# Latent attention: from a planned order to a fixed one

## The chip, the cores and the metric

The kernel runs on one core of a Trainium2 chip. The metric is the device time of one execution in microseconds (us).

## The reference, cut to what matters

The model is two blocks: an attention and recurrence block with its feed-forward part, and a second block of two layers (neighbourhood attention with a feed-forward part, then latent attention with a mixture of eight experts). The change lies in the latent attention, here for 256 tokens, 16 heads, 64 unrotated and 32 rotated dimensions of each query and key, 64 of each value:

```python
def _apply_rope(x, cos, sin):
    x1 = x[..., 0::2].astype(jnp.float32)
    x2 = x[..., 1::2].astype(jnp.float32)
    out = jnp.stack([x1 * cos - x2 * sin, x1 * sin + x2 * cos], axis=-1)
...
def _mla(h, w_down, q_norm, w_uq, kv_norm, w_ukv, w_o):
    down = h @ w_down
    c_q = _rmsnorm(down[..., :MLA_Q_LORA]) * q_norm
    c_kv = _rmsnorm(down[..., MLA_Q_LORA:MLA_Q_LORA + MLA_KV_LORA]) * kv_norm
    k_rope = down[..., MLA_Q_LORA + MLA_KV_LORA:]
    q = (c_q @ w_uq).reshape(B, S, MLA_HEADS, MLA_NOPE + MLA_ROPE)
    kv = (c_kv @ w_ukv).reshape(B, S, MLA_HEADS, MLA_NOPE + MLA_V)
    k_nope, v = kv[..., :MLA_NOPE], kv[..., MLA_NOPE:]
...
        s = (jnp.einsum('bqhd,bkhd->bhqk', qn, k_nope)
             + jnp.einsum('bqhr,bkr->bhqk', qr, k_rope)).astype(jnp.float32) * scale
        p = jax.nn.softmax(s, axis=-1).astype(v.dtype)
        return jnp.einsum('bhqk,bkhd->bqhd', p, v)
...
    return o @ w_o
```

## The kernel before

Matrices are multiplied as sums of three products: each float32 operand is split into a rounded high part (a copy on ScalarE) and the rest (a subtraction on VectorE). `split_to` does this for activations (L524), and `Stream.split` for weights (L98, L99): every weight slab of up to 128 x 1024 costs one ScalarE copy and one VectorE subtraction. `W.next()` hands out the next split slab and splits further ones ahead, into six buffers.

The 16 heads are treated in eight pairs, the 256 query rows in two tiles of 128 rows (`t`). For each pair the work is:

- `prepare`: for every second pair a projection of the queries of four heads (twelve matmuls of 384 columns into two `pb` banks, L486 to L489; copies to `qt` on ScalarE, L1149) and the rotation of their last 32 dimensions on VectorE (`turn`, L1068 to L1073, six instructions for each row tile). Then the keys of the pair (three matmuls, L1153 to L1155) and the transposes of the queries (four, L1162), both split with `split_to`.
- `scores`: six matmuls for each row tile into a `pa` bank (L699 to L701).
- `softmax_rows`, for each row tile: a row maximum for each head on VectorE (L643), the scaling of both (L644), the exponentials with their sums on ScalarE (L646), a reciprocal (L648) and a multiply for each head (L650) on VectorE.
- `turn_P`: eight transposes (L663) into `pb` and `pc` banks and two copies on ScalarE (L669).
- `pv`: eight matmuls (L676), split into `oT`.

`attention` writes these steps down in the order scores i, softmax i, prepare i + 2, turn i - 1, product with the values i - 1. Nothing holds the engines to that order: a planner orders the instructions of each engine by priority and by its own idea of when each can run, so that work of later steps and of other stages may be put between. In the stage of the experts the helper `in_order` ties the instructions of an engine to the order in which they are written; instructions written elsewhere may still be put between them. Behind the stage `out_proj` multiplies `oT` with the output weights: 96 matmuls of 512 columns that accumulate in all four `pa` banks. PSUM has four `pa` banks, two `pb` and two `pc`; `pbc` takes `pb` and `pc` in turn.

Of the kernel before, what the change touches and what calls it, by code (L numbers as in the profile page):

```python
# [19 lines left out]
S, D = 256, 1024  # L20
# [154 lines left out]
def consts():  # L175
# [8 lines left out]
    rope = np.stack([np.cos(ang), np.sin(ang)], 1).astype(np.float32)  # L184
# [4 lines left out]
def model(ctx: ExitStack, tc: tile.TileContext, A, out, cap=128):  # L189
# [443 lines left out]
    def softmax_rows(Ps, srcs, biases, scale):  # L633
# [4 lines left out]
        for i in range(n):  # L638
            if biases is not None:
                V.tensor_tensor_reduce(Ps[i], srcs[i], biases[i], scale=1.0, scalar=-3.0e38, op0=OP.add, op1=OP.max,  # L640
                                       accum_out=mx[:, i:i + 1])
            else:
                V.tensor_reduce(mx[:, i:i + 1], srcs[i], axis=AX.X, op=OP.max)  # L643
        V.tensor_scalar(mx, mx, -scale, None, OP.mult)  # L644
        for i in range(n):
            SC.activation(Ps[i], srcs[i] if biases is None else Ps[i], AF.Exp, bias=mx[:, i:i + 1], scale=scale,  # L646
                          accum_out=sums[:, i:i + 1])
# [8 lines left out]
    def turn_P(P, pt, causal, rev):  # L656
        for h in range(2):
            ps = pbc()
# [6 lines left out]
            if causal:  # L665
                V.tensor_copy(*run(pt[:, h, 0], ps[:, 0:256]))
                V.tensor_copy(*run(pt[:, h, 1, 128:256], p3[:, 1, 1]))
            else:
                SC.copy(*run(pt[:, h].rearrange("p k n -> p (k n)"), ps))  # L669
# [382 lines left out]
    with ExitStack() as ph:  # L1052
# [8 lines left out]
        SC.dma_start(rope, A["c_rope"].rearrange("(t p) u f -> p t u f", p=128))  # L1061
# [12 lines left out]

        with ExitStack() as ph2:
# [9 lines left out]
            for c0, c1, n in ((256, 384, 160), (0, 256, 256)):  # L1085
# [8 lines left out]
                for t in range(2):  # L1094
# [13 lines left out]
                    tmp = sm.tile([128, 4, 1, 16], F32, name="rt1")  # L1108
                    turn(dn[t][:, 384:416].rearrange("p (o n) -> p o n", o=1), 1, t, tmp)
# [27 lines left out]
        q = ph.enter_context(tc.tile_pool(name="mla2", bufs=2))  # L1137
        qTs = [pair(q, [128, 2, S], "qT") for _ in range(2)] + [(q3[:, 0], q3[:, 1])]
        qt = {}

        def prepare(i):
            if i % 2 == 0:
                w = W.next()
                acc = [[pb()], [pb()]]
                for kk in range(2):
                    tokmm(acc, cT, kk, w, kk == 0, kk == 1, halves=1, n=384, o=kk * 384)
                qt[0] = q.tile([128, 2, 4, 96], F32, name="qt")
                for t in range(2):
                    SC.copy(qt[0][:, t].rearrange("p h n -> p (h n)"), acc[t][0][:, :384])  # L1149
                    tmp = q.tile([128, 4, 4, 16], F32, name="rt4")  # L1150
                    turn(qt[0][:, t, :, 64:96], 4, t, tmp)
# [4 lines left out]
            k = kT[i % 3]  # L1156
            for h in range(2):
                split_to(k[0][0:64, h], k[1][0:64, h], ps[h * 64:h * 64 + 64, :256])
            pq = pbc()
            for h in range(2):  # L1160
                for t in range(2):
                    PE.transpose(pq[0:96, (h * 2 + t) * 128:(h * 2 + t + 1) * 128], qt[0][:, t, 2 * (i % 2) + h], ident)  # L1162
            qT = qTs[i % 3]
            split_to(qT[0][0:96], qT[1][0:96], pq[0:96].rearrange("p (h n) -> p h n", h=2))
            return qT, k
# [366 lines left out]
```

## Time and profile before

| | us |
|---|---|
| median of 3 runs | 1331.69 |
| lowest and highest of them | 1330.03 and 1334.1 |
| profiled execution, its own time | 1335.88 |
| span of the profiled execution | 1333.9 |
| TensorE busy in it | 1259.1 |
| VectorE busy in it | 1077.9 |
| ScalarE busy in it | 847.9 |

The profile is of one execution; its span is the time between its first and its last instruction. Times in it are us from the start of the span, and durations of single instructions are ns where a view says so. In the profile PE is TensorE's matmul, PEld its weight load, DVE VectorE, ACT ScalarE, POOL GpSimd, SP the engine that issues most loads. The latent attention lies between about 675 and 788 us of the span.

### The profile page before, as it was taken

How to read it: one execution, taken by the hardware profiler on the slowest of the kernel's cores; microseconds unless marked ns; L12 is line 12 of the kernel's file. 1: busy time of each engine (PE TensorE's matmuls, PEld its weight loads, DVE VectorE, ACT ScalarE, POOL GpSimd, SP SyncE). 2: the span in 40 equal slices, each digit the busy share in tenths (PEclk: the TensorE clock that was granted, in tenths of full speed). 3: DMA queues.
4: the chain of work that ended last, by engine and by line, in shares of the span. 5: the costliest groups of instructions: out<-in, count | busy, mean ns of one | idle time of the engine just before them, and what ended most of it. 6: DMA issues, size and time to landing. Idle time of an engine off the chain costs nothing. (4 is left out here: it accounts for less than half of the span.)

```text
span 1333.9 us, 20102 instructions
## 1 busy us (share of the span) xinstructions
PE 1259.1 (94%) x7459; PEld 1121.3 (84%) x7459; DVE 1077.9 (81%) x1761; ACT 847.9 (64%) x1354; POOL 36.2 (3%) x68
## 2 busy tenths in 40 slices
PE   7988999999999989999998988999999999999985
PEld 6966989999798779999987667889998988999873
DVE  6796699997787496878768867988888898888995
ACT  7874555555566554434447747777777787878872
POOL 4000000000100000000000020000000000000000
PEclk9999999999899989999979998999999999999997
DMA  9843599893685277899642145999999999999990
GB/s 329 301 142 125 150 386 338 294 323 111 203 271 174 80 284 260 315 382 346 226 140 91 30 141 190 390 362 353 369 380 348 354 378 377 336 355 390 376 347 34
DMA packets 190171, 359.56 MB, mean 270 GB/s; under 512 B 15460, under 2 KB 147970, under 8 KB 189937
## 3 DMA queue, kind: packets, MB, share of 16 engines
q1 hardware_dynamic: 187361, 351.70, 74.9%
q10 hardware_dynamic: 1584, 3.91, 0.7%
q0 software_dynamic: 1120, 2.58, 0.5%
q8 instruction: 61, 1.00, 0.3%
q14 instruction: 45, 0.37, 0.1%
HBM read 351.56 MB, written 7.06 MB: 269 GB/s over the span
## 5 line engine op out<-in xcount | busy, mean ns | idle before, releaser
L99 DVE TENSOR_TENSOR wlo<-raw,whi 128x1024 fp32r<-128x1024 f32 (+2 forms) x577 | 644.9, 1158 | 125.4 <-ACT whi L98 118.9
L98 ACT CAST whi<-raw 128x1024 fp32r<-128x1024 f32 (+2 forms) x577 | 557.5, 1003 | 115.8 <-PE pa L489 35.5
L1453 PE MATMUL pa<-wlo,xT 128*128 128x448 f32 x512 | 186.3, 364 | 3.3 <-DVE wlo L99 3.3
L1452 PE MATMUL pa<-whi,xT 128*128 128x448 f32 x512 | 188.4, 368 | 0.4 <-ACT whi L98 0.4
L1454 PE MATMUL pa<-whi,xT 128*128 128x448 f32 x512 | 185.5, 362 | 0.0
L289 DVE SCALAR_TENSOR_TENSOR acc<-raw,cact,acc 128x1024 f32<-128x1024 f32 x84 | 107.3, 1277 | 3.1 <-DMA raw<-in_w_ada_dram 2.9
L1453 PEld LDWEIGHTS pa<-wlo,xT 128*128 128x128 f32 x512 | 96.3, 188 | 10.9 <-DVE wlo L99 4.8
L1452 PEld LDWEIGHTS pa<-whi,xT 128*128 128x128 f32 x512 | 96.3, 188 | 7.4 <-ACT whi L98 0.7
L1454 PEld LDWEIGHTS pa<-whi,xT 128*128 128x128 f32 x512 | 96.1, 188 | 6.3
L486 PE MATMUL pb<-whi,hTh 128*128 128x512 f32 x224 | 88.6, 396 | 0.7 <-ACT hTh L524 0.7
L487 PE MATMUL pb<-wlo,hTh 128*128 128x512 f32 x224 | 88.8, 396 | 0.2 <-DVE wlo L99 0.2
L478 PE MATMUL pb<-hTh,whi 128*128 128x256 f32 x512 | 75.3, 291 | 0.3 <-ACT hTh L575 0.2
L478 PEld LDWEIGHTS pb<-hTh,whi 128*128 128x128 f32 x512 | 71.0, 197 | 5.1 <-ACT hTh L575 1.3
L478 PE MATMUL pb<-hTl,whi 128*128 128x256 f32 x512 | 72.9, 285 | 0.0
L478 PE MATMUL pb<-hTh,wlo 128*128 128x256 f32 x512 | 72.8, 286 | 0.0
L489 PE MATMUL pb<-whi,hTl 128*128 128x512 f32 x224 | 70.1, 395 | 1.6 <-DVE hTl L524 1.6
L486 PE MATMUL pa<-whi,fh 128*128 128x512 f32 x176 | 69.6, 395 | 0.0
L487 PE MATMUL pa<-wlo,fh 128*128 128x512 f32 x176 | 69.2, 393 | 0.0
L478 PEld LDWEIGHTS pb<-hTl,whi 128*128 128x128 f32 x512 | 66.9, 194 | 0.0
L478 PEld LDWEIGHTS pb<-hTh,wlo 128*128 128x128 f32 x512 | 66.8, 194 | 0.1
L478 PE MATMUL pc<-hTh,whi 128*128 128x256 f32 x448 | 63.8, 285 | 2.4 <-ACT whi L98 2.4
L478 PE MATMUL pc<-hTl,whi 128*128 128x256 f32 x448 | 63.7, 286 | 0.0
(433 smaller groups left out, 2081.4 us busy)
## 6 DMA issues: line engine op xcount, KB each, us to landing
raw<-in_moe_w_gu_dram SPq DMA_DIRECT2D x128, 896.0 KB, 7.6
raw<-in_moe_w_down_dram SPq DMA_DIRECT2D x56, 1024.0 KB, 6.7
raw<-in_w_ada_dram SPq DMA_DIRECT2D x48, 1024.0 KB, 7.5
raw<-in_w_up_dram SPq DMA_DIRECT2D x22, 1024.0 KB, 9.9
raw<-in_ffn_w_gu_dram SPq DMA_DIRECT2D x22, 1024.0 KB, 6.2
raw<-in_na_w_qkv_dram SPq DMA_DIRECT2D x12, 1024.0 KB, 5.0
raw<-in_w_down_dram SPq DMA_DIRECT2D x11, 1024.0 KB, 4.8
raw<-in_ffn_w_down_dram SPq DMA_DIRECT2D x11, 1024.0 KB
```

The costliest lines, as they stand in the source:

```text
L98: self.last = self.nc.scalar.copy(h, src)
L99: self.nc.vector.tensor_sub(l, src, h.bitcast(F32))
L289: V.scalar_tensor_tensor(ada_acc[0], raw, cact[:, k:k + 1], ada_acc[0], op0=OP.mult, op1=OP.add)
L478: PE.matmul(ps, lhsT=w[:, k], rhs=x[:, k], start=n + k == 0, stop=n == 2 and k == KD - 1)
L486: PE.matmul(acc[t][j][:, :n], lhsT=xh, rhs=ws[j][0], start=first, stop=False)
L487: PE.matmul(acc[t][j][:, :n], lhsT=xh, rhs=ws[j][1], start=False, stop=False)
L489: PE.matmul(acc[t][j][:, :n], lhsT=xl, rhs=ws[j][0], start=False, stop=last)
L1452: PE.matmul(ps, lhsT=xh, rhs=wh, start=k == 0, stop=False)
L1453: PE.matmul(ps, lhsT=xh, rhs=wl, start=False, stop=False)
L1454: PE.matmul(ps, lhsT=xl, rhs=wh, start=False, stop=k == KD - 1)
```

## The change

The stage gets a function of its own, `pairs`, whose instructions on TensorE, ScalarE and VectorE are tied to the order in which they are written (`in_order`). That order differs from before: the P of the pair before is turned ahead of the scores of the next, in two `pa` banks; the product with the values stands last. The queries of four heads are projected and rotated four pairs ahead of their scores, that is two pairs ahead of their own transposes (the first two projections before the loop). The maxima of both row tiles stand ahead of the normalising, one instruction for two heads, already negated; the scale is multiplied into the queries when they are split. The reciprocals and multiplies of tile 0 stand before the preparation of pair i + 2, those of tile 1 behind it, and then the rotation and the rests of the splits. A rotation is three instructions for both row tiles, with tables that hold each cosine twice and each sine with both signs; GpSimd writes the sines out for four heads. P has three buffers in a pool of its own, and the turned P is written into P's own tile.

```diff
-    rope = np.stack([np.cos(ang), np.sin(ang)], 1).astype(np.float32)
+    rope = np.stack([np.repeat(np.cos(ang), 2, -1), np.stack([-np.sin(ang), np.sin(ang)], -1).reshape(S, 32)], 1)
+    rope = rope.astype(np.float32)
...
-    def turn_P(P, pt, causal, rev):
+    def turn_P(P, pt, causal, rev, bank=None):
         for h in range(2):
-            ps = pbc()
+            ps = (bank or pbc)()
...
-                SC.copy(*run(pt[:, h].rearrange("p k n -> p (k n)"), ps))
+                SC.copy(pt[:, h], ps.rearrange("p (k n) -> p k n", k=2))
...
-        rope = p.tile([128, 2, 2, 16], F32, name="rope")
+        rope = p.tile([128, 2, 2, 32], F32, name="rope")
+        rope4 = p.tile([128, 2, 4, 32], F32, name="rope4")
+        rt4 = p.tile([128, 2, 2, 4, 32], F32, name="rt4")
...
+        GP.tensor_copy(rope4, rope[:, 1, :, None, :].to_broadcast([128, 2, 4, 32]))
...
-        def turn(x, n, t, tmp):
-
-            x1, x2 = x[:, :, 0::2], x[:, :, 1::2]
-            cs, sn = (rope[:, t, u][:, None, :].to_broadcast([128, n, 16]) for u in range(2))
-            V.tensor_mul(tmp[:, 0], x1, cs)
-            V.tensor_mul(tmp[:, 1], x2, sn)
-            V.tensor_mul(tmp[:, 2], x1, sn)
-            V.tensor_mul(tmp[:, 3], x2, cs)
-            V.tensor_sub(x1, tmp[:, 0], tmp[:, 1])
-            V.tensor_add(x2, tmp[:, 2], tmp[:, 3])
+        def turn(x, n, cs, sn, a, b):
+
+            pairs = lambda y: y.rearrange("p t n (f u) -> p (t n) f u", u=2)
+            V.tensor_mul(a, x, cs[:, :, None, :].to_broadcast([128, cs.shape[1], n, 32]))
+            V.tensor_mul(pairs(b), pairs(x)[:, :, :, ::-1], pairs(sn))
+            V.tensor_add(x, a, b)
...
+        def queries(i):
+
+            w = W.next()
+            acc = [[pb()], [pb()]]
+            for kk in range(2):
+                tokmm(acc, cT, kk, w, kk == 0, kk == 1, halves=1, n=384, o=kk * 384)
+            x = qt[i // 2] = q.tile([128, 2, 4, 96], F32, name="qt")
+            for t in range(2):
+                SC.copy(x[:, t].rearrange("p h n -> p (h n)"), acc[t][0][:, :384])
+            return lambda: turn(x[:, :, :, 64:96], 4, rope[:, 0], rope4, rt4[:, 0], rt4[:, 1])
+
         def prepare(i):
...
+            for h in range(2):
+                SC.copy(k[0][0:64, h], kps[h])
+            SC.activation(qT[0][0:96], p3, AF.Copy, scale=96 ** -0.5)
+
+            def rests():
+                for h in range(2):
+                    V.tensor_sub(k[1][0:64, h], kps[h], k[0][0:64, h].bitcast(F32))
+                V.scalar_tensor_tensor(qT[1][0:96], p3, 96 ** -0.5, qT[0][0:96].bitcast(F32), op0=OP.mult,
+                                       op1=OP.subtract)
+            return (qT, k), rests
...
-        attention(8, prepare, scores, softmax, v, oT, q, lead=2)
+        def pairs():
+            qk, Ps = {}, {}
+            for i in (0, 2):
+                queries(i)()
+            for i in (0, 1):
+                qk[i], rests = prepare(i)
+                rests()
+            for i in range(9):
+                if i >= 1:
+                    pt = Ps[i - 1].rearrange("p t h n -> p h t n")
+                    turn_P(Ps[i - 1], pt, False, 0, pa)
+                if i < 8:
+                    sc = scores(i, qk.pop(i))
+                    P = Ps[i] = qP.tile([128, 2, 2, 256], F32, name="P")
+                    mx, sums = ([sm.tile([128, 2], F32, name=x) for _ in range(2)] for x in ("mx", "sums"))
+                    for t in range(2):
+                        V.tensor_reduce(mx[t], sc[t].rearrange("p (h n) -> p h n", h=2), axis=AX.X, op=OP.max,
+                                        negate=True)
+                        for h in range(2):
+                            SC.activation(P[:, t, h], sc[t][:, h * 256:(h + 1) * 256], AF.Exp, bias=mx[t][:, h:h + 1],
+                                          accum_out=sums[t][:, h:h + 1])
+
+                    def normalise(t):
+                        V.reciprocal(sums[t], sums[t])
+                        for h in range(2):
+                            V.tensor_scalar(P[:, t, h], P[:, t, h], sums[t][:, h:h + 1], None, OP.mult)
+
+                    normalise(0)
+                rotate = queries(i + 4) if i % 2 == 0 and i < 4 else None
+                rests = None
+                if i + 2 < 8:
+                    qk[i + 2], rests = prepare(i + 2)
+                if i < 8:
+                    normalise(1)
+                if rotate:
+                    rotate()
+                if rests:
+                    rests()
+                if i >= 1:
+                    pv(pt, v, (i - 1) * 128, oT, i - 1, False)
+
+        with in_order(PE, SC, V):
+            pairs()
```

## Rows read from the trace of the kernel before

**Rows 1.** Windows: start:end, length, each engine's busy us (instructions), clock, DMA.

```profile
716.40:770.50 54.10, 50.16 (x321) 38.11 (x321) 44.36 (x165) 40.12 (x117) 0.00 (x0) 1.00 0.11 35
770.50:788.20 17.70, 17.70 (x79) 14.67 (x79) 7.48 (x15) 5.50 (x10) 0.65 (x3) 1.00 0.48 156
...
800.00:805.00 5.00, 1.23 (x5) 1.14 (x5) 4.13 (x25) 0.83 (x2) 1.29 (x1) 0.50 0.04 15
```

**Rows 2.** Groups by form, VectorE, 707.8 to 770.6: busy us, mean ns | idle before.

```profile
L643 DVE TENSOR_REDUCE mx<-pa 128x1 f32<-128x256 f32 x32 | 12.3, 414 | 1.1 <-PE pa L701 0.9
L650 DVE TENSOR_SCALAR P<-P,sums 128x256 f32<-128x256 f32 x32 | 9.6, 344 | 0.0
L99 DVE TENSOR_TENSOR wlo<-raw,whi 128x1024 fp32r<-128x1024 f32 x5 | 6.1, 1217 | 0.0
L524 DVE TENSOR_TENSOR qTl<-pc,qTh 96x512 fp32r<-96x512 f32 x4 | 2.7, 678 | 0.0
...
L524 DVE TENSOR_TENSOR ol<-pb,oh 128x256 fp32r<-128x256 f32 x4 | 1.7, 423 | 2.2 <-ACT oh L524 2.2
```

**Rows 3.** Groups by form, ScalarE, 707.8 to 770.6.

```profile
L98 ACT CAST whi<-raw 128x1024 fp32r<-128x1024 f32 x6 | 6.4, 1059 | 0.0
L669 ACT COPY pt<-pc 128x512 f32<-128x512 f32 x8 | 4.7, 592 | 1.3 <-PE pc L663 1.2
```

**Rows 4.** By tile, rotation: ns min/median/max, first and last start, forms.

```profile
L1070 DVE TENSOR_TENSOR rt<-qt,rope x8: 211/218/223, 712.5 to 749.6; 128x64 f32<-128x64 f32 x8
...
L1068 DVE TENSOR_TENSOR rt<-h,rope x2: 175/176/176, 697.2 to 699.7; 128x16 f32<-128x16 f32 x2
...
L1061 ACTq DMA_DIRECT2D rope<-in_c_rope_dram x1: 445/445/445, 675.4 to 675.4; - x1
```

**Rows 5.** Timeline, weight loads in front of TensorE's matmuls: start us, us.

```profile
739.40 0.46 PEld L663 LDWEIGHTS pb<-ident,P 128*128 128x128 f32 x4
...
740.26 0.19 PEld L701 LDWEIGHTS pa<-k1h,qTl 96*128 96x128 f32 x1
...
741.33 0.19 PEld L1153 LDWEIGHTS pc<-cTh,wnh 128*128 128x128 f32 x1
...
743.15 0.19 PEld L676 LDWEIGHTS pb<-pt,v 128*64 128x64 f32 x2
...
744.58 0.19 PEld L486 LDWEIGHTS pb<-whi,cTh 128*128 128x128 f32 x1 [0.39 <-DVE mx L644]
...
746.61 0.53 PEld L663 LDWEIGHTS pc<-ident,P 128*128 128x128 f32 x4
```

**Rows 6.** Timeline, handoffs of the softmax: start us, us.

```profile
759.60 0.49 ACT L646 ACTIVATE P<-pa,mx 128x256 f32<-128x256 f32 x1
...
760.95 0.50 ACT L646 ACTIVATE P<-pa,mx 128x256 f32<-128x256 f32 x1
...
761.31 0.23 ACT L646 ACTIVATION_READ_ACCUMULATOR P<-pa,mx 128x1 f32 x1
761.39 0.28 PE L701 MATMUL pa<-k1h,qTl 96*128 96x256 f32 x1
...
761.72 0.43 DVE L643 TENSOR_REDUCE mx<-pa 128x1 f32<-128x256 f32 x1 [0.88 <-PE pa L701]
...
763.49 0.17 DVE L644 TENSOR_SCALAR mx<-mx 128x2 f32<-128x2 f32 x1
...
763.75 0.47 ACT L646 ACTIVATE P<-pa,mx 128x256 f32<-128x256 f32 x1 [1.95 <-DVE mx L644]
...
766.69 0.17 DVE L648 RECIPROCAL sums<-sums 128x2 f32<-128x2 f32 x1 [0.85 <-ACT P L646]
...
766.89 0.62 DVE L650 TENSOR_SCALAR P<-P,sums 128x256 f32<-128x256 f32 x2
```

**Rows 7.** Timeline, the first query projection goes on; the output projection is done.

```profile
711.93 0.19 PEld L486 LDWEIGHTS pb<-whi,cTh 128*128 128x128 f32 x1
...
788.09 0.14 PEld L1200 LDWEIGHTS pb<-ident,xres 128*128 128x128 f32 x1
```

More of the change, by code (lines that the diff above doesn't have):

```diff
@@ L638, in softmax_rows @@
         for i in range(n):
[L639 to L643, printed above, removed]
+            V.tensor_tensor_reduce(Ps[i], srcs[i], biases[i], scale=1.0, scalar=-3.0e38, op0=OP.add, op1=OP.max,
+                                   accum_out=mx[:, i:i + 1])
         V.tensor_scalar(mx, mx, -scale, None, OP.mult)
         for i in range(n):
-            SC.activation(Ps[i], srcs[i] if biases is None else Ps[i], AF.Exp, bias=mx[:, i:i + 1], scale=scale,
+            SC.activation(Ps[i], Ps[i], AF.Exp, bias=mx[:, i:i + 1], scale=scale,
                           accum_out=sums[:, i:i + 1])
@@ L1107, in model @@
                     V.tensor_copy(dn[t][:, 384:416], acc[t][0][:, 128:160])
-                    tmp = sm.tile([128, 4, 1, 16], F32, name="rt1")
-                    turn(dn[t][:, 384:416].rearrange("p (o n) -> p o n", o=1), 1, t, tmp)
+                    tmp = sm.tile([128, 2, 1, 32], F32, name="rt1")
+                    turn(dn[t][:, 384:416].rearrange("p (t o n) -> p t o n", t=1, o=1), 1, rope[:, 0, t:t + 1],
+                         rope4[:, t:t + 1, 0:1], *(tmp[:, u:u + 1] for u in range(2)))
                     PE.transpose(ps[0:32, 128:256], dn[t][:, 384:416], ident)
@@ L1137, in model @@
         q = ph.enter_context(tc.tile_pool(name="mla2", bufs=2))
+        qP = ph.enter_context(tc.tile_pool(name="mlaP", bufs=3))
         qTs = [pair(q, [128, 2, S], "qT") for _ in range(2)] + [(q3[:, 0], q3[:, 1])]
         qt = {}
-        def prepare(i):
[L1142 to L1151, printed above, removed]
+        def queries(i):
[7 more added lines that the diff above has]
+            return lambda: turn(x[:, :, :, 64:96], 4, rope[:, 0], rope4, rt4[:, 0], rt4[:, 1])
+        def prepare(i):
             ps = pbc()
@@ L1155, in prepare @@
             PE.matmul(ps[:, :256], lhsT=wn[1][:, i * 128:(i + 1) * 128], rhs=cT[0][:, 2], start=False, stop=True)
-            k = kT[i % 3]
-            for h in range(2):
-                split_to(k[0][0:64, h], k[1][0:64, h], ps[h * 64:h * 64 + 64, :256])
             pq = pbc()
@@ L1161, in prepare @@
                 for t in range(2):
[L1162 to L1165, printed above, removed]
+                    PE.transpose(pq[0:96, (h * 2 + t) * 128:(h * 2 + t + 1) * 128], qt[i // 2][:, t, 2 * (i % 2) + h],
+                                 ident)
+            k, qT = kT[i % 3], qTs[i % 3]
+            kps = [ps[h * 64:h * 64 + 64, :256] for h in range(2)]
+            p3 = pq[0:96].rearrange("p (h n) -> p h n", h=2)
+            for h in range(2):
[7 more added lines that the diff above has]
+            return (qT, k), rests
         def scores(i, qk):
@@ L1176, in scores @@
             return res
-        def softmax(i, sc, P):
-            for t in range(2):
-                softmax_rows([P[:, t, h] for h in range(2)], [sc[t][:, h * 256:(h + 1) * 256] for h in range(2)],
-                             None, 96 ** -0.5)
-        attention(8, prepare, scores, softmax, v, oT, q, lead=2)
+        def pairs():
[38 more added lines that the diff above has]
+            pairs()
     r2 = moe_ph.enter_context(tc.tile_pool(name="r2c", bufs=MOE_SLOTS))
```

2 lines of the change are left out of this document (1 added, 1 removed).

## The prediction

> **What bounds the kernel now.** I read the stage by windows first [rows 1]. From the first scores of the latent attention (716.4 us) to its last product (770.5 us) TensorE is busy for 50.16 of 54.10 us by the profile's modelled ends, VectorE for 44.36, ScalarE for 40.12; TensorE's clock is whole (1.00), and DMA does little (0.11). No engine is full and none is far from it, so what counts is the order in which they hand work to each other. Then the groups by form, for what one instruction costs on VectorE [rows 2] and ScalarE [rows 3]; the view by tile for the rotation [rows 4]; and the timeline for the spacing on TensorE [rows 5] and the handoffs of the softmax [rows 6]. Behind the stage the output projection runs densely to 788.09 us [rows 7], 79 matmuls in 17.70 us [rows 1], 0.224 us each. Of its 96 matmuls 18 were thus done in gaps of the last pairs. Everything later starts from there, so I take a shift of 788.09 one to one to the end.
>
> **TensorE's pieces, per pair of heads** [rows 5]. Eight transposes of P: 739.40 to 740.26, 0.86. Scores: nine matmuls from 740.26 to 741.33, 0.119 each, so twelve are 1.43 and one row tile 0.71. Keys: three of these, 0.36. Query transposes: four, 0.43. P times V: 743.15 to 744.58, 1.43 with the pause behind it. A query projection for two pairs: 744.58 to 746.61, 2.03. An ordinary pair needs 4.51 us of TensorE, one with a projection 6.54.
>
> **VectorE's pieces** [rows 2, 4]. A maximum over 256 columns takes 0.414, a subtraction over 1024 takes 1.217: 1.05 ns per column, so one maximum over two heads (512) comes to 0.68. Two multiplies of 0.344 span 0.62 [rows 6], so each instruction holds the engine 0.07 less than its duration. Then: maxima 2 x 0.61 in place of 4 x 0.34 and two scalings; normalising 2 x 0.55; rests of keys and queries 0.34 + 0.34 + 0.61 = 1.29; rest of the output 0.35. A rotation was 12 instructions of 0.218, 1.8 us; it becomes 3 over 256 columns of about 0.42, 1.05 us. The scale folded into the query split replaces one pass by one pass. So VectorE has less to do, some 0.3 us per pair and 0.75 per rotation. That alone is worth nothing unless VectorE holds up the chain.
>
> **Costed at nothing.** The wider rope table and POOL's copy of its sines: the load is issued at 675.4 and first used at 697.2 [rows 4], 21.8 us of cover for 64 KB. POOL's later copies queue behind it and have the same cover. If that were gone, the first rotation would wait, and with it the keys. The three P buffers replace P and pt; the turned P lies in P's own tile, written only after the transposes that read it.
>
> **The new chain of one pair.** The order on TensorE is now: turn pair i-1, scores of i, projection, keys and queries of i+2, P times V of i-1. Turning waits for the second half of the normalising, and scores wait behind turning. From the start of turning: transposes 0.86; five matmuls to the last of tile 0, 0.60; to the maximum 0.33 (761.39 to 761.72); the maximum 0.68; to the first exponential 0.09 (763.66 to 763.75); four exponentials with their sums 1.94 (759.60 to 761.54); reciprocal to multiply 0.20 (766.69 to 766.89); multiply 0.34; to the transposes 0.10, as for the other handoff [rows 6]. Sum 5.14; the first transpose needs tile 0 alone, so 0.11 comes off: **5.03 us per pair**, above TensorE's 4.51. VectorE's queue behind the last multiply (free at 5.25, rests 1.29, output 0.35) runs to 6.89, 1.86 into the next pair, whose maximum wants it at 1.79: 5.10 in pairs with rests.
>
> **The two pairs that project queries (0 and 2).** The projection brings a weight split with it: on ScalarE 1.06 [rows 3] behind the exponentials, 4.37 to 5.43; then 1.15 on VectorE, between the two halves of the normalising. The second half starts at 6.83, the next turning at 7.16. In pair 0 the rotation (1.05) and rests then run VectorE to 9.72, 2.56 into pair 1, which is 0.77 late. In pair 2 TensorE decides: the projection holds both pb banks until ScalarE has copied them, behind its split, at about 5.9; keys and query transposes start at 6.0, P times V ends at 8.22. Loop: 7.16 + 5.80 + 8.22 + 5.09 + 3 x 5.10 + 5.03 = **46.6 us**.
>
> **The prologue** now holds two projections. TensorE gets on with the first at 711.93 [rows 7], nine matmuls left, to 713.5; its copies free the banks by 714.2; the second ends at 715.9 and is copied at 716.6; VectorE rotates to 717.7, then has the rests of pairs 0 and 1 ahead of the first maximum, to 720.2. Turning would start 1.79 earlier: virtual start 718.4.
>
> **The sum.** 718.4 + 46.6 = 765.0: the last pair is turned. Transposes, two copies of P (0.59 each [rows 3], the second done at 1.75) and P times V end 3.2 later, 768.2. The projection's accumulators lie in the banks of the last scores and of the last turned P, so fewer of its matmuls fit into gaps: some 9, four behind the last scores and four or five under the copies. 87 x 0.224 = 19.5, end 787.7. The planner may still put foreign instructions between the ordered ones. Two weight splits of the output projection find free buffers once the projections are over; each can stand 1.15 us in VectorE's way. From below 0 (they fall into holes), from above 2.3; I take 1.0. 788.7 against 788.09: **+0.6 us**. The profiled span of 1333.9 would be 1334.5, its own time 1335.88 would be 1336.5. The median of the runs shown is 4.2 us under that run, so the forecast is 1331.69 + 0.6 = 1332.3. A difference under 0.3% (4 us) counts as none.
>
> The terms not shown by the trace: the merged maximum is bounded by 0.41 (one of 256) and 0.83 (two), the rotation pass by 0.22 and 1.22; the values taken lie on the line between rows. Handoffs are the short ends of their rows, so the loop is nearer its lower end. A shorter loop is bounded by TensorE alone (second rival).
>
> **Rivals.**
> *As summed, no change* (0.62). For it: 54.1 us with three projections and 18 foreign matmuls stands against 46.6 + 3.2 with two and nine; what leaves the loop comes back in the prologue and behind it. Its own range is -3.5 to +5 us.
> *TensorE sets the pace* (0.18). If turning finds P ready, the loop is TensorE's own 6 x 4.51 + 2 x 6.54 = 40.1, 6.5 less: 1325.8. For it: TensorE is at 93% before. Against: it needs 0.5 us out of a chain with no parallel branch.
> *Pauses, slower* (0.16). Behind P times V TensorE stands 0.39 before the next load [rows 5]. In a fixed order nothing else can be slipped in; if two more such pauses come on the chain in each pair (before the turned P and before the scores), 8 x 0.76 = 6 us: 1338.4. It decides from 0.5 us per pair. Against: scores follow transposes at 740.26 without a pause.
> *The clock falls* (0.04). Around 800 to 805 us, with TensorE nearly idle, the granted clock was 0.50, the lower level of 1.2 GHz [rows 1]. Each pair has some 0.5 us without matmuls, pairs 0 and 2 about 1.5. Two stretches of 5 us at the lower level would delay up to 5 us: 1337.
> The Trainium skill, TensorE: Matmul & The Clock Gate, "A second HAM failure mode: psum-queue depth-cycling", says that many short idle moments between groups of matmuls can make the clock swing between its levels. By it the forecast would be this rival's 1337, by the row of the loop 1332.3; the trace of before, with short gaps throughout the loop and a granted clock of 1.00, does not agree.
>
> **How the numbers follow.** The likeliest gives 1332.3. The range 1325.5 to 1338.5 leaves out the far ends of the second and third rival. Faster by over 0.3%: three quarters of the second and a twentieth of the first, 0.17. Slower: most of the third and fourth and a twelfth of the first, 0.21. Same: 0.62.
>
> **What would show it.** Turning to turning 5.0 to 5.3 us in pairs 3 to 7, some 7.2 in pair 0, 8 in pair 2; the first maximum near 720; the first maximum of a pair released by TensorE, the transposes by the second multiply; a merged maximum of 0.68 and rotation passes of 0.42; the last P times V ending near 768; about 87 projection matmuls behind it. The prediction is wrong if the prologue's first scores come before 717 or after 721, if a pair takes under 4.7 or over 5.6, or if VectorE's weight subtractions stand between maximum and reciprocal in most pairs.

## The result: slower by 8 us

The changed kernel takes 1340.89 us (median of four executions, 1339.93 to 1342.0); the kernel before, in its four executions, takes 1332.75. The ratio is 1.0065, 95% interval 1.0049 to 1.008: slower by more than the 0.3% that counts, and above the predicted range (1325.5 to 1338.5). The profiled execution took 1340.03 us, with a span of 1338.2.

The two profiled executions can't be laid on each other from zero, since the work ahead of the latent attention ended at different times. I align them at the last transpose of a modulation vector, ahead of the stage. Timeline of the kernel before: that transpose and the first maximum (the end of its stage stands in [rows 7]).

```profile
683.26 0.38 PE L316 MATMUL pc<-ident,adac 128*8 128x128 f32 x1
...
718.92 1.09 DVE L643 TENSOR_REDUCE mx<-pa 128x1 f32<-128x256 f32 x3
...
788.32 0.93 PE L1200 MATMUL pb<-ident,xres 128*128 128x128 f32 x7
```

The same marks in the changed kernel, and between them the transposes that turn the last pair:

```profile
678.14 0.38 PE L317 MATMUL pc<-ident,adac 128*8 128x128 f32 x1
...
716.17 1.27 DVE L1203 TENSOR_REDUCE mx<-pa 128x2 f32<-128x512 f32 x2
...
766.11 0.98 PE L661 MATMUL pa<-ident,P 128*128 128x128 f32 x7 [0.84 <-DVE P L1212]
...
790.83 1.03 PE L1246 MATMUL pb<-ident,xres 128*128 128x128 f32 x8
```

From these rows, and from the spans 1333.9 and 1338.2, in us (the predicted column follows from the prediction's 720.2, 765.0 and 788.7; 0.11 is added to the second, because 766.11 is the second transpose of its turning, and 0.23 to the third, because 788.32 stands 0.23 behind the mark of [rows 7]):

| stretch | before | predicted | after |
|---|---|---|---|
| last modulation transpose to first maximum | 35.66 | 36.9 | 38.03 |
| first maximum to the last pair's turning | - | 44.9 | 49.94 |
| turning to the routing's first transposes | - | 23.8 | 24.72 |
| (the last two together) | 69.40 | 68.7 | 74.66 |
| routing to the end | 545.6 | 545.6 | 547.4 |
| sum | 650.7 | 651.3 | 660.1 |

So four stretches are off: +1.1, +5.0, +0.9 and +1.8 us, the second most of all. Windows of the changed kernel (columns as in [rows 1]): the three stretches, the stage as a whole, and two places inside the loop.

```profile
678.14:716.17 38.03, 33.31 (x207) 28.15 (x207) 30.12 (x77) 22.25 (x49) 3.25 (x5) 0.91 0.55 184
716.17:766.11 49.94, 38.55 (x265) 31.52 (x264) 39.23 (x99) 37.37 (x111) 0.00 (x0) 0.93 0.12 38
766.11:790.83 24.72, 24.71 (x112) 19.46 (x112) 8.11 (x18) 7.74 (x13) 0.63 (x3) 1.00 0.34 112
...
716.17:790.83 74.66, 63.26 (x376) 50.97 (x375) 47.34 (x116) 45.10 (x124) 0.63 (x3) 0.95 0.19 62
...
742.00:744.00 2.00, 1.67 (x9) 1.48 (x10) 1.92 (x7) 0.78 (x2) 0.00 (x0) 0.74 0.56 115
744.00:746.00 2.00, 2.00 (x11) 2.00 (x11) 1.22 (x3) 0.59 (x1) 0.00 (x0) 0.50 0.90 344
760.00:762.00 2.00, 2.00 (x12) 2.00 (x11) 0.20 (x1) 1.17 (x2) 0.00 (x0) 0.51 0.00 0
762.00:764.00 2.00, 2.00 (x12) 1.72 (x13) 1.03 (x2) 0.79 (x3) 0.00 (x0) 0.64 0.00 0
```

In the loop TensorE is busy for 38.55 of 49.94 us (77%); before it was 93% [rows 1]. And the granted clock, 1.00 throughout the loop of before, fell to the lower level (0.50) twice. The view of waits of the changed kernel over the loop (us in total, times, longest) names who waits for whom:

```profile
ACT P L1206 <- DVE mx L1203: 10.1, 9, 2.1
PE pa L661 <- DVE P L1212: 8.4, 12, 2.5
...
DVE mx L1203 <- PE pa L699: 4.1, 4, 2.2
```

It is a ring: exponentials wait for maxima, turning for the normalised probabilities, maxima for scores. VectorE's groups by form in the loop answer to [rows 2]: single instructions cost what was forecast (a merged maximum 681 ns, 0.68 predicted), so the time lies between them.

```profile
L1203 DVE TENSOR_REDUCE mx<-pa 128x2 f32<-128x512 f32 x16 | 10.4, 681 | 4.1 <-PE pa L699 4.1
L1212 DVE TENSOR_SCALAR P<-P,sums 128x256 f32<-128x256 f32 x32 | 9.8, 349 | 0.5
L99 DVE TENSOR_TENSOR wlo<-raw,whi 128x1024 fp32r<-128x1024 f32 x4 | 4.9, 1215 | 2.1 <-ACT whi L98 2.1
```

The longest wait of TensorE, 2.5 us, has its cause in VectorE's timeline in pair 3:

```profile
737.98 1.28 DVE L1203 TENSOR_REDUCE mx<-pa 128x2 f32<-128x512 f32 x2
739.18 1.21 DVE L99 TENSOR_TENSOR wlo<-raw,whi 128x1024 fp32r<-128x1024 f32 x1
740.31 0.15 DVE L1210 RECIPROCAL sums<-sums 128x2 f32<-128x2 f32 x1
740.38 1.20 DVE L99 TENSOR_TENSOR wlo<-raw,whi 128x1024 fp32r<-128x1024 f32 x1
741.50 0.60 DVE L1212 TENSOR_SCALAR P<-P,sums 128x256 f32<-128x256 f32 x2
```

Two weight splits of the output projection stand between the maxima and the first multiply. TensorE has nothing to do until that multiply is done; the first fall of the clock follows. Pair 3 took 7.4 us from turning to turning where 5.09 was forecast.

### The profile page after: what moved, and what is told of

Read it like the earlier page. It is cut to its first block, busy times and chain, and to the rows that moved or that the text cites. A ratio compares the mean times of both kernels' runs of the same rounds, so it can differ in the third digit from the quotient of the medians.

```text
span 1338.2 us, 20052 instructions
## 1 busy us (share of the span) xinstructions
PE 1251.7 (94%) x7459; PEld 1116.4 (83%) x7459; DVE 1074.9 (80%) x1687; ACT 848.4 (63%) x1354; POOL 36.6 (3%) x69
## 5 line engine op out<-in xcount | busy, mean ns | idle before, releaser
L479 PEld LDWEIGHTS pb<-hTh,whi 128*128 128x128 f32 x512 | 70.3, 196 | 6.2 <-ACT hTh L576 1.9
L479 PE MATMUL pc<-hTh,wlo 128*128 128x256 f32 x448 | 63.0, 283 | 0.0
```

What stands on the lines that cost most here:

```text
L479: PE.matmul(ps, lhsT=w[:, k], rhs=x[:, k], start=n + k == 0, stop=n == 2 and k == KD - 1)
```

## Experiments

Fifteen kernels ran, in four groups on three chips, each beside the kernel before on the same chip. Runs of one kernel lie 2 to 11 us apart, the longer ones mostly with a lower mean clock, so I give for each, from its profiled execution, the three stretches of the table above (to the first maximum, from there to the routing, behind it), and from all its executions the mean granted clock and the ratio to before. The intervals are 0.003 to 0.004 wide, so a difference of 0.002 between two kernels isn't clear of noise by the ratios alone.

| kernel | to maximum | stage | behind | clock | ratio (95%) |
|---|---|---|---|---|---|
| before | 35.66 | 69.40 | 545.6 | 0.971 to 0.972 | 1 |
| changed | 38.03 | 74.66 | 547.4 | 0.970 | 1.0065 (1.0049 to 1.008) |
| e1, splits behind | 38.01 | 70.27 | 547.4 | 0.968 | 1.0053 (1.0039 to 1.0067) |
| e2, busy TensorE | 39.20 | 72.34 | 547.4 | 0.969 | 1.0051 (1.0036 to 1.0067) |
| e3, both | 38.03 | 70.28 | 547.9 | 0.970 | 1.006 (1.0047 to 1.0073) |
| e4, planned order | 41.21 | 65.87 | 544.2 | 0.970 | 1.0001 (0.9987 to 1.0015) |
| e5, scores first | 40.53 | 70.02 | 547.7 | 0.968 | 1.0026 (1.0014 to 1.0039) |
| e6, shorter VectorE work | 36.56 | 68.11 | 545.0 | 0.969 | 1.0002 (0.9988 to 1.0016) |
| e7, code moved | 38.02 | 73.12 | 545.5 | 0.970 | 1.0055 (1.0039 to 1.0071) |
| e8, old banks | 40.52 | 74.57 | 546.4 | 0.968 | 1.0055 (1.0035 to 1.0075) |
| e9, gap filled | 38.00 | 69.29 | 545.8 | 0.969 | 1.0026 (1.001 to 1.0042) |
| e10, before at the edge | 35.67 | 69.42 | 547.3 | 0.971 | 1.0015 (1.0001 to 1.0029) |
| e11, free TensorE | 37.36 | 69.54 | 545.0 | 0.970 | 1.0034 (1.0018 to 1.0049) |
| e12, splits and code | 40.52 | 70.53 | 547.4 | 0.967 | 1.0047 (1.0028 to 1.0065) |
| e13, shorter work, busy | 37.22 | 68.63 | 545.0 | 0.973 | 0.9985 (0.997 to 1.0) |
| e14, before, busy | 36.86 | 70.73 | 545.6 | 0.971 | 1.0012 (0.9998 to 1.0027) |
| e15, splits, code, busy | 38.56 | 70.50 | 545.2 | 0.972 | 1.0025 (1.0008 to 1.0043) |

My first theory was: the two foreign splits and the two falls of the clock. The rival: the fixed order itself.

**e1, splits behind.** The next stage's weight splits are held back until the last exponential and the last multiply.

```diff
...
                     pv(pt, v, (i - 1) * 128, oT, i - 1, False)
+            W.behind(fs, fv)
```

> The weight splits of the output projection and of the experts are held back until the last exponential and the last multiply of pair 7; nothing else is changed against the changed kernel. Theory (foreign splits and the clock): the two subtractions that stood in VectorE's queue in pair 3 are gone, pair 3 takes 5.3 us in place of 7.4, TensorE's wait of 2.5 us goes and with it the first fall of the clock, so pair 4 takes 5.3 in place of 6.45; about 3.3 us less than the changed kernel, some 1337.5 us. The second fall (pair 7) stays. Rival (the fixed chain itself costs the 8 us, the splits only lay in its holes): no difference to the changed kernel, 1341 us. Second rival: held back, the splits are late for the output projection and cost there what they save here.

**e2, busy TensorE.** Transposes of the identity ahead of turning in the two pairs before whose turning the clock fell, into columns that the turned P overwrites.

```diff
...
-                    turn_P(Ps[i - 1], pt, False, 0, pa)
+                    turn_P(Ps[i - 1], pt, False, 0, pa, {4: (20, 3), 7: (8, 5)}.get(i, (0, 0)))
```

> Transposes whose result is overwritten at once (23 before the turned P of pair 3, 13 before that of pair 6) stand in the two long waits of TensorE; the splits stay where they are. Theory (the clock is a cause of its own): the granted clock stays at 1.00 in pairs 4 and 7, pair 4 takes 5.3 us in place of 6.45 and pair 7 5.2 in place of 6.45, about 2.4 us less than the changed kernel, 1338.5 us; pair 3 stays at 7.4. Rival (the rows at half clock only stretch work that waits anyway): no difference, or up to 0.5 us more for the added work.

**e3, both** (the fill only at the second place).

> The splits are held back and the wait of pair 6 is filled (13 transposes whose result is overwritten). Theory: both falls of the clock and the two foreign subtractions are gone, all pairs from 3 on take 5.1 to 5.3 us; 4.6 us less than the changed kernel, 1336.3 us, which leaves about 3.5 us over the kernel before, for the prologue and the projection matmuls that no longer fit into gaps. Rival (chain alone): 1341 us.

**e4, planned order.** The changed kernel without the fixed order.

```diff
-        with in_order(PE, SC, V):
-            pairs()
+        pairs()
```

> The changed kernel without the tie of the engines to the written order; the steps are written down as in the changed kernel and the planner orders them. Theory (a fixed order leaves holes that nothing may fill and foreign work that it does not see): the planner puts scores and projections into the holes, the granted clock stays at 1.00, the stage comes back to within 2 us of the kernel before or under it: 1329 to 1335 us. Rival (what costs is not the tie but the place of the steps, turned P in the banks of the scores and the product with the values last): 1338 to 1342 us, no difference.

In its own trace e1 shortens the stage by 4.4 us, e2 by 2.3. e1 has no fall of the clock inside the loop. e2 has none at the two filled places, but one in pair 0, which the trace of the changed kernel doesn't have:

```profile
724.00:728.00 4.00, 4.00 (x24) 3.79 (x23) 3.71 (x11) 2.50 (x5) 0.00 (x0) 0.57 0.00 0
```

e3 is no shorter than e1 (70.28 and 70.27): the second fall, which it was to mend, is missing in e1 as well, although TensorE waits 1.03 us there too. Windows of e1, first maximum to turning, then to the routing:

```profile
720.26:766.37 46.11, 35.49 (x264) 28.45 (x263) 37.19 (x97) 35.56 (x110) 0.00 (x0) 1.00 0.07 21
766.37:790.53 24.16, 24.16 (x111) 19.45 (x112) 10.47 (x20) 9.25 (x15) 0.64 (x3) 1.00 0.45 153
```

The loop is now 46.1 and the rest 24.2, near the forecast's 44.9 and 23.8. But over all executions only 1 to 2 us came back, with intervals that overlap that of the changed kernel, while e4 took away all of it. Window of e4, first maximum to routing:

```profile
723.68:789.55 65.87, 60.75 (x371) 48.13 (x369) 44.10 (x114) 42.83 (x122) 0.63 (x3) 1.00 0.19 62
```

Without the fixed order the same steps take 8.8 us less in the stage. So the theory holds for the loop that was traced and not for the time: the rival stands, and two things were still hidden, one in each column beside the stage.

**e7, code moved.** Behind the stage the changed kernel, e1, e2 and e3 take 1.8 to 2.3 us more than the kernel before, and all four wait at the very end. There a branch jumps over an overflow path that is never taken, and the last normalisation follows. ScalarE's first square root there, in the changed kernel:

```profile
1330.33 0.48 ACT L508 ACTIVATE ry<-ssx,re 128x1 f32<-128x1 f32 x2 [5.23 <-issue]
```

and in the kernel before:

```profile
1326.67 0.48 ACT L507 ACTIVATE ry<-ssx,re 128x1 f32<-128x1 f32 x2 [3.22 <-DVE re L505]
```

"issue" says that it waited for no engine. The edit adds four instructions to the path that is not taken:

```diff
         with tc.If(rv > cap):
+            pad = sm.tile([128, 1], F32, name="warm")
+            for _ in range(4):
+                SC.copy(pad, epsc)
```

> The changed kernel with four one-element-wide copies on ScalarE added inside the branch at the end that is never taken; what is executed stays the same, only the code behind the branch stands four instructions further on. In the traces so far with the fixed order, ScalarE's first instruction behind the branch comes at once and the second 2.3 us later, with an instruction transfer between them; in the kernel before the second follows after 0.23 us. Theory A (this gap is a piece of code that is fetched late because a block of code ends just there): the gap falls to about 0.2 us and the stretch from the branch to the end shortens by 2.0 us; time 2 us below the changed kernel, ratio to before about 1.005 (1.0065 without the move). Theory B (the gap belongs to the work and not to the place of the code): gap and time stay, ratio about 1.0065.

```profile
1331.31 0.48 ACT L508 ACTIVATE ry<-ssx,re 128x1 f32<-128x1 f32 x2 [3.14 <-DVE re L506]
```

The wait for "issue" is gone and the stretch behind the stage is 1.95 us shorter: theory A in the trace. The ratio fell by 0.001, where 0.0015 was expected, within the noise. (e4's trace has no wait for "issue" either, so about 2 us of its gain come from the place of the code and not from the order.)

**e10, before at the edge.** The reverse: the same edit in the kernel before, with eleven instructions.

> The kernel before with eleven one-element-wide copies on ScalarE added inside the branch at the end that is never taken, so that ScalarE's code behind the branch stands where it stood in the changed kernel. Nothing else differs and nothing more is executed. Theory A (the place of the code decides): ScalarE's second instruction behind the branch comes 2.2 us after the first instead of 0.23, and the time is 2.1 us longer, ratio 1.0016. Theory B (the gap belongs to the changed kernel's order): no gap, ratio 1.000.

```profile
1329.04 0.48 ACT L507 ACTIVATE ry<-ssx,re 128x1 f32<-128x1 f32 x2 [5.19 <-issue]
```

The gap came, the stage stayed the same to 0.02 us, and the ratio is 1.0015: 2 us that have nothing to do with attention. The Trainium skill, Runtime: NRT & Kernel Launch, "Instruction fetch mechanics", says that a taken branch whose target lies outside the pages of code at hand breaks the prefetch and stalls for a fetch. The trace agrees in kind, with 3.1 to 3.2 us idle behind the branch and ahead of the square root, and e7 and e10 add a second stall of 2 us that comes and goes with the place of the code. That a block of code ends just there is an inference that no run shows.

**e8, old banks** (with the moved code). The turned probabilities go back to the banks of before.

```diff
-                    turn_P(Ps[i - 1], pt, False, 0, pa)
+                    turn_P(Ps[i - 1], pt, False, 0)
```

> As the kernel with the moved code, and the turned probabilities go back to the PSUM banks that they had before instead of those of the scores and of the output projection. Theory A (the projection lost its fill-ins because its banks are taken by the turned probabilities): eight or more of the projection's 96 matmuls run inside the loop again instead of two or three, and the stretch from the last turning to the end of the projection shortens by 1 to 1.7 us; ratio 1 to 1.5 thousandths below that of the moved code. Theory B (they are lost because TensorE's order is fixed and serial): no more than three fill-ins, ratio within 0.5 thousandths of the moved code; if the old banks make the turning wait for the key and query transposes, up to 2 us slower.

Seven of the projection's matmuls came back into the loop (theory A had eight or more), but the stage was no shorter (74.57, with two falls of the clock in it) and the ratio is that of e7. Theory A's mechanism, nearly, without its gain.

**e5, scores first** (with the moved code and the splits held back).

```diff
...
+                if i < 8:
+                    sc = scores(i, qk.pop(i))
                 if i >= 1:
                     pt = Ps[i - 1].rearrange("p t h n -> p h t n")
                     turn_P(Ps[i - 1], pt, False, 0, pa)
                 if i < 8:
-                    sc = scores(i, qk.pop(i))
...
```

> As the kernel with the moved code, the weight splits of the next stage held behind the last pair, and in the fixed order the scores of a pair stand ahead of the turning of the pair before, the turning ahead of the maxima's successors. Theory A (the loop is long because turning, scores, maximum, exponential and multiply of one pair after another form one chain; ordinary pair 5.29 us): pairs of 4.6 to 4.8 us, loop 43 us instead of 51.6, stage 4 us shorter than with the splits held back alone, time 1329 to 1332 where the kernel before takes 1334, ratio 0.996 to 0.999. Theory B (VectorE and ScalarE's own busy time, about 5 us a pair, sets the pace, whatever the order): pairs of 5.1 to 5.3 us, ratio 1.002 to 1.004.

Its maxima come at 745.74, 751.03, 756.32 and 761.62: pairs of 5.29 us, as in the changed kernel. So the chain through TensorE isn't the pace (theory B, as the ratio of 1.0026 has it). VectorE's timeline in e1, one ordinary pair:

```profile
747.36 1.27 DVE L1203 TENSOR_REDUCE mx<-pa 128x2 f32<-128x512 f32 x2
749.18 0.17 DVE L1210 RECIPROCAL sums<-sums 128x2 f32<-128x2 f32 x1 [0.55 <-ACT P L1206]
749.39 0.62 DVE L1212 TENSOR_SCALAR P<-P,sums 128x256 f32<-128x256 f32 x2
...
750.83 0.85 DVE L1171 TENSOR_TENSOR k0l<-pc,k0h 64x256 fp32r<-64x256 f32 x2
751.70 0.69 DVE L1172 SCALAR_TENSOR_TENSOR qTl<-pb,qTh 96x512 fp32r<-96x512 f32 x1
752.31 0.41 DVE L525 TENSOR_TENSOR ol<-pc,oh 128x256 fp32r<-128x256 f32 x1
```

The next maximum starts at 752.64, with no gap but the 0.55 behind the maxima: VectorE has 4.74 us of work a pair, and in the fixed order must stand still while ScalarE does the first exponentials.

**e12, splits and code.** e1 with the moved code, as the base for the next two.

> The changed kernel with both mends that had an effect so far: the next stage's weight splits held behind the last pair, and the code behind the untaken branch moved by four instructions. The traces give 74.7 us from the first maximum to the first transposes of the routing in the changed kernel, 70.3 with the splits held back, and 13.0 against 10.9 us from the branch to the end. Theory A (these are two separate costs): 70.3 and 10.9 us in the profile, ratio 1.0065 less 0.0021 for the splits and 0.0016 for the code: 1.003. Theory B (the time of the splits comes back behind the stage): ratio 1.005 as with the moved code alone.

Its stage (70.53) and the missing wait for "issue" are as in theory A, but the ratio of 1.0047 is nearer to theory B's 1.005. The reasons that its trace shows stand behind e11.

**e9, gap filled.** VectorE's half of the output split goes into that gap.

```diff
...
+            SC.copy(oT[0][:, i], ps[:, :256])
+            later.append(lambda: V.tensor_sub(oT[1][:, i], ps[:, :256], oT[0][:, i].bitcast(F32)))
...
+                    while later:
+                        later.pop()()
                     normalise(0)
```

> As the kernel with both mends, and VectorE's half of splitting a pair's output (0.41 us) moved from the end of its pair into the gap of 0.55 us behind the next pair's maxima. Theory A (an ordinary pair is VectorE's own 4.74 us of work and one round trip to ScalarE of 0.55 us): the pair shortens from 5.29 to 4.88 us, the loop by 2.5 to 3 us, ratio 0.002 below that of both mends. Theory B (the period is TensorE's, or ScalarE's): the gap only grows elsewhere, the pair stays at 5.2 to 5.3 us and the ratio where it was.

```profile
747.61 1.41 DVE L1207 TENSOR_REDUCE mx<-pa 128x2 f32<-128x512 f32 x2
748.94 0.41 DVE L680 TENSOR_TENSOR ol<-pb,oh 128x256 fp32r<-128x256 f32 x1
749.45 0.17 DVE L1214 RECIPROCAL sums<-sums 128x2 f32<-128x2 f32 x1
...
752.70 0.69 DVE L1207 TENSOR_REDUCE mx<-pa 128x2 f32<-128x512 f32 x1
```

The pair is 5.09 us (747.61 to 752.70), 0.20 shorter and not 0.41. The stage is 1.2 us shorter than that of e12, 1.0 shorter than that of e1, and the ratio 0.002 below e12's, with intervals that overlap: between the theories. What is left fits the chain of 5.03 to 5.10 us that the prediction summed.

**e11, free TensorE.** The fixed order on ScalarE and VectorE alone.

```diff
-        with in_order(PE, SC, V):
+        with in_order(SC, V):
```

> As the kernel with both mends, with the fixed order on ScalarE and VectorE alone; TensorE's order is left to the planner. Theory A (the fixed order on TensorE keeps the projection's matmuls out of the loop): ten or more of them move into the loop, the stretch behind the last turning shortens by 1.5 to 3 us, ratio 0.001 to 0.002 below that of both mends. Theory B (the order of VectorE and ScalarE is what leaves TensorE waiting, and the projection finds its places or not by its banks): no more than three move, ratio within 0.0005 of both mends.

Three of the projection's matmuls now stand ahead of the last turning; in the kernel before it is sixteen. Theory B by the count; the ratio is 0.0013 below e12's, within the noise. But the fixed order isn't what keeps the projection out: e4, with no fixed order, has three as well and takes the time of before. With the turned P in its old banks seven stand there, in the fixed order (e8) and in the planner's (e6).

e12's profiled execution shows what spreads the runs. Its loop is nearly as short as that of e1 (46.4 us), but its first maximum comes 40.52 us behind the mark. Windows of e12:

```profile
704.00:706.00 2.00, 1.02 (x5) 0.49 (x3) 1.90 (x9) 2.00 (x6) 1.08 (x2) 1.00 1.04 307
...
708.00:710.00 2.00, 0.79 (x5) 0.43 (x4) 1.67 (x5) 0.52 (x1) 0.51 (x1) 1.00 0.17 70
710.00:712.00 2.00, 2.00 (x15) 2.00 (x13) 0.00 (x0) 1.73 (x3) 0.00 (x0) 0.67 0.04 8
712.00:714.00 2.00, 2.00 (x9) 1.74 (x9) 0.50 (x2) 0.12 (x1) 0.00 (x0) 0.50 0.00 0
```

TensorE is half idle in two of three windows, then the clock falls, and the query projections that the change has put ahead of the loop run at half speed: +2.5 us. The same fall stands in e4, e5 and e8 (to maximum 40.5 to 41.2), in part in e2, and not in the others. The idle time alone doesn't decide it: e1 has TensorE busy for 0.98 and 1.02 us in 704 to 706 and 708 to 710, and keeps 1.00.

Behind the stage e12 has no wait for "issue" and still takes 547.4 us. Near the end its clock is lower for longer than that of the changed kernel, one window of each:

```profile
1314.08:1324.08 10.00, 7.85 (x26) 5.77 (x25) 4.48 (x6) 3.09 (x4) 0.00 (x0) 0.83 0.01 2
```

```profile
1310.83:1320.83 10.00, 7.27 (x27) 5.09 (x27) 5.67 (x7) 3.99 (x6) 0.00 (x0) 0.95 0.01 2
```

The traces of the kernel before, e5 and e8 have the 0.83 too. From the last matmul of the experts on tile `xT` to ScalarE's last sum ahead of the branch these four take 22.6 us, all others 20.8 to 21.0.

**e15, splits, code, busy.** e12 with transposes of the identity in those waits.

```diff
                     if c0 == 0:
+                        for _ in range(8):
+                            PE.transpose(ps[:, 0:128], ident, ident)
...
             pq = pbc()
+            for _ in range(8 if i == 0 else 0):
+                PE.transpose(pq[:, 0:128], ident, ident)
```

> As the kernel with both mends, and 24 transposes of the identity matrix on TensorE in the waits ahead of the first maximum (eight ahead of each turning of the normalised query rows, eight ahead of the first queries' transposes), into PSUM columns that are overwritten. Theory A (TensorE's idle stretches there bring the fall of the clock at 710 us): no fall between 700 and 730 us, first maximum 38 us behind the last modulation transpose, mean granted clock of the runs 0.970 or more, ratio 0.0015 below that of both mends (1.0047), thus about 1.003. Theory B (the falls come in any case): a fall in the trace or a mean clock below 0.969, and the ratio of both mends or 1 us above it.

```profile
704.00:706.00 2.00, 1.64 (x12) 1.15 (x11) 1.91 (x7) 1.32 (x5) 0.72 (x3) 1.00 0.88 277
...
708.00:710.00 2.00, 2.00 (x16) 1.75 (x14) 1.36 (x5) 0.78 (x2) 0.00 (x0) 1.00 0.04 12
710.00:718.00 8.00, 7.46 (x46) 6.33 (x47) 3.89 (x9) 5.46 (x10) 0.00 (x0) 1.00 0.00 0
```

No fall at 710 (one remained at 727), mean clock 0.972 against 0.967, ratio 0.002 lower. Theory A by ratio and mean clock, with two cautions: the intervals overlap, and the fall at 727 is one that theory B names.

**e6, shorter VectorE work** in the planner's order: the kernel before with the merged negated maxima, the scale in the queries and the three-instruction rotation.

```diff
+                V.tensor_reduce(mx, sc[t].rearrange("p (h n) -> p h n", h=2), axis=AX.X, op=OP.max, negate=True)
...
+        attention(8, prepare2, scores, softmax, v, oT, q, lead=2)
```

> The kernel before with only the shorter VectorE work of the change: one negated maximum for both heads, the scale in the queries, the rotation in three instructions; the order is again left to the planner, queries are projected with their own pair and each half is normalised at once. Theory A (what costs is the fixed order, and the shorter work is a gain of its own): 2 to 4 us below the kernel before, ratio 0.997 to 0.9985. Theory B (VectorE isn't what the stage waits for, so shorter work moves nothing): within 1 us of before, ratio 0.999 to 1.001. Theory C (merging the maxima delays the first exponential of each pair): 2 us above before, ratio 1.0015.

Theory B in the time, 1.0002. The stage is 1.3 us shorter, with one fall of the clock in it, and the first maximum 0.9 later.

**e14, before, busy** and **e13, shorter work, busy.** The kernel before, and e6, with e15's transposes (for the first two query groups).

> The kernel before with the same transposes of the identity ahead of the first maximum, eight of them ahead of the transposes of each of the first two query groups. Theory A (the kernel before has no falls there to lose): the same time, ratio 0.9995 to 1.0005, or up to 1 us more for the transposes themselves. Theory B (it has falls in a part of its runs as well): 1 us less, ratio 0.999, and a mean clock above 0.972.

> The shorter VectorE work in the planner's order, as tried, with the same transposes of the identity as in the kernel before. In its trace the stage from the first maximum to the routing took 68.1 us with one fall of the clock (3.4 us at half clock), against 69.4 without a fall in the kernel before. Theory A (without falls the shorter work is a gain): no fall in the stage, 66.5 us, ratio 0.997 to 0.9985. Theory B (TensorE's own work sets this stage, with a fall or without): ratio 0.9995 to 1.001.

e14 is 0.0012 above before, with an interval that takes in 1, and its clock is no higher, so theory B's gain didn't come. In its trace the first maximum comes 1.2 us later, more than was allowed for the transposes. e13 is the only kernel below before, 0.9985, with an interval that touches 1. Its clock is the highest of all (0.973), but its traced stretches (37.22 and 68.63) sum to 0.8 us more than those of before. The windows from the first maximum to the routing, before and e13, show why the shorter work gives so little:

```profile
718.92:788.32 69.40, 65.46 (x382) 50.30 (x381) 49.53 (x176) 44.82 (x125) 0.65 (x3) 1.00 0.21 67
```

```profile
719.98:788.61 68.63, 66.22 (x391) 51.68 (x390) 46.24 (x118) 44.59 (x125) 0.63 (x3) 1.00 0.21 68
```

VectorE lost 3.3 us of work, TensorE is busy for 94 and 96% of the stage (in e13 a few of the added transposes count in). In the planner's order TensorE is nearly all that the stage consists of, with sixteen of the projection's matmuls in its gaps in the one and seven in the other.

## Why the prediction was wrong

The sum, +0.6 us, was wrong by 8.8 us in the traces. By its steps:

**The loop of 46.6 us is the step that failed** (+5.0). It let nothing foreign and no fall of the clock into the loop; the 1.0 us for foreign splits was added behind it. By its own sign it was wrong where a pair took over 5.6 us: pair 3 took 7.4, pairs 4 and 7 took 6.45 each. Shown: holding the splits back takes 2.3 us out (e7 to e1: 48.45 to 46.11 from first maximum to turning, the fall behind pair 3 included), the second fall cost 1.5 (changed to e7, which waits as long at that place and keeps its clock: 49.94 to 48.45), and 1.2 are left (46.11 against 44.9). Of these an ordinary pair holds 0.19, 5.29 for 5.10: the terms were right, but VectorE's idle time behind the maxima was not counted, because VectorE's queue was measured from turning and not around its own ring; e9 took the idle time out and the pair fell to 5.09. Pair 0 (7.03 for 7.16, from 1.79 us ahead of the first maximum as in the prediction), pair 1 (6.02 for 5.80) and pair 2 (7.7 for 8.22) were near. The rival *pauses* forecast a slower kernel, but from at least 0.5 us in every pair; an ordinary pair lost 0.19.

**The order itself.** Holding the splits back leaves a stage of 70.3 us without a fall of the clock (e1), and the planner does the same steps in 65.9 (e4). These 4.4 us belong to the fixed order, less what e4 has done ahead of its first maximum, which comes 3.2 us later, some 2.5 of them by a fall of the clock as in e12. The 0.19 us a pair are a part of them; where the rest lies was not taken apart. The prediction summed the fixed chain alone and didn't ask what the planner would make of the same steps.

**"The clock falls" had 0.04** and came twice in the trace, behind TensorE waits of 2.5 and 1.0 us. Its evidence was the clock of 1.00 in the loop of before, with TensorE at 93%; the changed loop has 77%. That share alone doesn't bring the falls: e1 has the same 77% (35.49 of 46.11 us) and none. The wait of 2.5 us was followed by a fall in both traces that have it (changed, e7), the wait of 1.0 us in the changed kernel only, not in e1 and e7. And e2, e5, e8, e11, e12 and e15 have a fall in pair 0 or 1 that the changed kernel's trace lacks. The rule cited there (the Trainium skill, TensorE: Matmul & The Clock Gate, "A second HAM failure mode: psum-queue depth-cycling") has the clock swing under many short idle moments; the trace of after agrees only in part, with two falls to 0.50, each behind one wait of 1.0 us or more. It was not the main term: the traces of e1 and e3 have no fall in the stage, and over all executions both are still at 1.005 and 1.006.

**A shift one to one to the end** failed by 1.8 us. Shown by e7 and e10: code behind a branch moved by eleven instructions, and that costs 2 us in either kernel. The 1.8 is a net figure: near the end the trace of the kernel before is 1.6 us longer, at a lower clock, than that of the changed kernel (22.6 against 21.0 above), and what else the changed kernel lost behind the stage was not taken apart.

**The prologue** was 1.1 us short also where no clock fell. What of it is waiting I did not take apart. That two projections ahead of the loop also lie open to a fall of the clock (some 2.5 us more in three traces of the fixed order and in that of e4) was not seen at all.

**The projection.** "Some 9" of its matmuls ahead of the last product were two, both behind the last pair's turning; with the 1.0 us for the splits that never came there, the stretch was off by 0.9 only. The reason given, the banks, is a part of it (e8: seven came back). The fixed order isn't the other part, since e4 has three and e6 seven without it; what brings the kernel before to sixteen stays open. Nor are the lost places what costs the time: e4 lost most of them and is level with before.

**Right** were the durations (0.68 for the merged maximum, 0.42 for a rotation pass), the shape of the first pairs, the last product 3.3 us behind the turning (3.2), and the sentence that shorter VectorE work is worth nothing by itself (e6: 1.0002).

**What stays open.** The terms make 8.8 us behind the mark for the traced execution; over all executions the mends of splits and code give back only a part (e12 1.0047), and transposes that keep TensorE busy perhaps another (e15 1.0025). How often the clock falls in each place can't be read from one traced execution of each kernel. And that e13's median lies below that of the kernel before isn't clear of noise; its mean clock is higher, its traced stretches are not shorter.

## What to carry to other kernels

Before an order written by hand replaces a planner's, take the busy share of the fullest engine over the stage: here TensorE was at 94%, so shorter work on VectorE had little to give (e6, e13), and an order that leaves TensorE idle for a quarter of the loop has much to lose. Run the same steps once without the fixed order: e4 showed in one run what the order costs. Walk each engine around its own ring and not only along the chain, and put in whatever a planner may still slip between: two splits of 1.2 us between maximum and multiply cost 2.3 us of the loop, the fall of the clock behind them included. When the end of a kernel moves although its stage did not, look for a first instruction behind a branch that waited for "issue".

## What was not expected of the hardware

The place of code behind a taken branch: ScalarE's second instruction behind the branch waited 2 us more or less, depending on four (e7) or eleven (e10) instructions that are never executed. And the clock: at half for the query projections behind a stretch in which TensorE was busy for 1.02 and 0.79 of two windows of 2 us, in some executions and not in others (e12 and e1 differ only in the never executed copies, and e1 kept 1.00 behind 0.98 and 1.02).
